# Moving the modulation products of a two-block, two-layer network between the feed-forward stages

## The chip, the cores and the metric

One core of a Trainium2 chip runs the whole program; TensorE (PE), VectorE (DVE), ScalarE (ACT), GpSimd (POOL) and SyncE (SP, which issues nearly all DMAs here) each work through a queue of their own. The metric is the device time of one execution in microseconds (us), smaller is better.

## The reference, cut to what matters

A first block of two layers (a state-space mixer with attention, memory attention, an FFN) works on 512 tokens of 1024 features; a second block of two layers works on its output `x` and on 256 context tokens. In the second block each layer's norms, gates and shifts are modulated by vectors that depend on the two conditioning vectors alone, and not on `x`:

```python
silu_c = jax.nn.silu(c)
silu_cc = jax.nn.silu(c_ctx)
for i in range(DEPTH):                      # DEPTH = 2
    mod = silu_c @ w_mod[i] + b_mod[i]      # w_mod[i]: 1024 x 6144
    mod_c = silu_cc @ w_mod[i] + b_mod[i]
    sh1, sc1, gt1, sh2, sc2, gt2 = jnp.split(mod[:, None, :], 6, axis=-1)
    ...
    h = modulate(rmsnorm_2(x, g_attn[i]), sh1, sc1)
    ...                                     # attention of this layer
    h = modulate(rmsnorm_2(x, g_ffn[i]), sh2, sc2)
    x = x + gt2 * conv_ffn(h, ...)
    if not last:
        ctx = ctx + gt2c * conv_ffn(hc, ...)   # the same weights, 256 columns
```

Both blocks' FFNs have 2816 hidden features: an up product to 5632, a three-tap convolution over positions, a gate, a down product. In the second block's first layer the FFN runs over `x` (512 columns) and the context (256 columns) with the same weights.

## The kernel before, in words

Everything is held feature-major: a tile is 128 features by 512 tokens. A float32 product is made of three passes: weights and activations are split into a high part and a low part, and `lin` (L304) runs high by high, high by low and low by high for each 128 rows. So 1024 input features by 512 columns are 24 matmuls, into one PSUM bank. `wload` loads a weight tile (`wr`, two buffers, issued by SP), ScalarE makes its high part (`wh`, three buffers, L314) and VectorE its low part (`wl`, three buffers, L331).

The modulation is not done on TensorE. `mod_steps(i, n0, n1)` is a generator: it loads the conditioning vectors (spread over all partitions) and takes their Silu, and then for each of 48 output tiles m and 2 halves e of the input loads 128 x 512 of `w_mod` and multiplies it with each of the two vectors. Of every eight products two are made on VectorE, which sums along the row in the same instruction (L1280); six are made on GpSimd (L1282), and ScalarE sums them later (L1260), `MLAG` products behind. Loads run `MPF` steps ahead. At the end of a layer's 96 steps the sums, the bias and the gains are put together in `mod[i]` and `G[i]`. In each layer i of the first block the generator of that layer is stepped by `step`: once for each output tile of the memory attention (`MSTEP[1]`), and after each up pair j of the FFN (`F1_MOD`: 2 in the first of the FFN's four parts, 5 in the others); what is left is run at the end of the FFN. So layer 0's modulation lies in the first block's first FFN and layer 1's in its second. These two stages are called the first FFNs here. `mod[0]` is first needed where the context is modulated at the end of layer 1's FFN.

The first FFNs (`ffn1`) work through 22 pairs j of up tiles (a value and a gate tile, 24 matmuls each), whose banks go around three tags L, S and PT of two banks each. The down products of a part are spread between the up products of the next one. For each up tile VectorE multiplies the bank with the norm, ScalarE does one tap, VectorE two more (L1181), then come Silu, the gate and the split.

The second block's FFN (`ffn2`) has three parts of 8, 7 and 7 pairs. In a part all up products come first: for each pair j, tile e and stream s (context, then `x`) a `lin` into a bank of tag L (two banks; four with S for the first two pairs), and `conv`: ScalarE copies the bank, VectorE does all three taps (L2021 and L2023). After the part's last gate the eight output tiles of the down product follow for both streams (L2080 adds them to `x` and the context). At the end of layer 0's, `mod[1]` and `G[1]` are needed for the norm of layer 1.

Activations, modulation weights and products all share one set of 59 buffers (tag A). The order of the instructions within an engine is set by a planner from the order in the program and the buffers and data that are free.

Of the kernel before, what the change touches and what calls it, by code (L numbers as in the profile page):

```python
# [14 lines left out]
AF = mybir.ActivationFunctionType  # L15
# [19 lines left out]
SA = 'g'  # L35
SQT = 'sq'
PSTEP = (5,3,1)
MSTEP = (0,1,4,1,2)
MDN = (0,0,2)
MH = 48  # L40
MLAG = 3
FX = 1
FD = 3
MK = 2
# [15 lines left out]
EV3 = 1  # L60
EV2 = 1
PIN = 1
MPF = 4
MODV = (0,4)
WP = 0
FA0 = 1
# [18 lines left out]
LAGS = (3,5)  # L85
FF_PARTS = ((0, 8), (8, 7), (15, 7))
F1_PARTS = ((0, 6), (6, 6), (12, 5), (17, 5))
F1_MOD = (2, 5, 5, 5)
F1_KEEP = 2
FTAGS = ("L", "S", "PT")  # L90

# [167 lines left out]
class Builder:  # L259
# [802 lines left out]
    def mem_attn(self, i, f, mh, K, fn):  # L1062
        nc, a = self.nc, self.a
        rm = []
        o = []
        qs, pts = {}, {}

        V = []

        def prep(h, ds=(0, 1)):  # L1070
            for d in ds:
                ps = self.p("L")
                self.lin(ps, self.wload(a[f"w_mq{i}"][2 * h + d]), f.rhs)
                if not rm:
                    rm.append(self.rstd_of(f.acc, D))
                t = self.t("A", [P, S])
                nc.vector.scalar_tensor_tensor(out=t, in0=ps, scalar=256.0 ** -0.5, in1=rm[0], op0=ALU.mult, op1=ALU.mult)
                qs[h, d] = self.split(t)

        self.steps = self.mod_steps(i, 0, 96)  # L1080
        mv = self.mem_v(i, mh, V)
        for h in range(2):
            for d in range(2):
                next(mv)
                next(mv)
                prep(h, (d,))
                self.step(2 * h + d, MSTEP[0])
        next(mv, None)

        def unit(h, qt):  # L1090
            u = Builder.Feed()
            s = slice(qt * P, qt * P + P)

            def s1():
                sp = self.p("S")
                for d in range(2):
                    kh, kl = K[2 * h + d]
                    qh, ql = qs[h, d]
                    self.mm(sp[:, :ML], qh[:, s], kh, d == 0, False)
                    self.mm(sp[:, :ML], qh[:, s], kl, False, False)  # L1100
                    self.mm(sp[:, :ML], ql[:, s], kh, False, d == 1)
                self.sm1(u, sp[:, :ML], ML)

            def s2():
                self.sm2(u, ML)
                if EV3:
                    turned()

            def turned():
                if qt % 2 == 0:  # L1110
                    pts[h, qt // 2] = self.t("A", [P, 2, 2, P], F32R), self.t("A", [P, 2, 2, P], F32R)
                ph, pl = (z[:, :, qt % 2] for z in pts[h, qt // 2])
                v = u.pt[:, :ML].rearrange("p (k q) -> p k q", k=2)
                self.hi(ph, v)
                self.lo(pl, v, ph)

            def s3():
                if not EV3:
                    turned()
                if qt < 3:  # L1120
                    return
                for d in range(2):
                    op = self.p("O")
                    c0 = (2 * h + d) * P
                    for hf in range(2):
                        oh = op[:, hf * ML:hf * ML + ML]
                        for kb in range(2):
                            vh, vl = V[c0 // 512][kb]
                            cs = slice(c0 % 512, c0 % 512 + P)
                            ph, pl = (z[:, kb].rearrange("p a q -> p (a q)") for z in pts[h, hf])  # L1130
                            self.mm(oh, vh[:, cs], ph, hf == 0 and kb == 0, False)
                            self.mm(oh, vh[:, cs], pl, False, False)
                            self.mm(oh, vl[:, cs], ph, False, hf == 1 and kb == 1)
                    o.append(self.split(op))

            return s1, s2, s3

        units = [unit(h, qt) for h in range(4) for qt in range(4)]
        self.pipe(units, {4 * h: (lambda h=h: prep(h)) for h in range(2, 4)}, 5, *XLAGS)
        for m in range(KD):  # L1140
            ps = self.p("L")
            self.lin(ps, self.wload(a[f"w_mo{i}"][m]), o)
            self.mark_d = nc.vector.tensor_add(out=self.x[:, m], in0=self.x[:, m], in1=ps)
            self.feed(fn, m)
            self.step(m, MSTEP[1])


    def step(self, n, r):
        for _ in range(int((n + 1) * r) - int(n * r)):
            with self.after(PIN):  # L1150
                next(self.steps, None)
# [3 lines left out]
    def ffn1(self, i, f, fn):  # L1155
# [2 lines left out]
        rf = []  # L1158
        self.wp = WP
        self.bank = 0  # L1160

        def bank():
            self.bank += 1
            return self.p(FTAGS[self.bank % len(FTAGS)])

        def up(j):
            ab = []
            for e in range(2):
# [72 lines left out]
        self.G = [[self.c([P, KD, 2], name=f"G{i}{j}") for j in range(2)] for i in range(DEPTH)]  # L1241


    def mod_steps(self, i, n0, n1):
        nc = self.nc
        cv = []
        for v in range(2):
            for e in range(2):
                c = self.t("A", [P, 512])
                nc.sync.dma_start(out=c, in_=self.a["cvec"][v, e])  # L1250
                nc.scalar.activation(c, c, AF.Silu)
                cv.append(c)
            yield
        part = self.mparts
        late = []

        def add(k):
            while len(late) > k:
                o, t = late.pop(0)
                nc.scalar.activation(t, t, AF.Copy, accum_out=o)  # L1260

        ws = {}

        def load(n):
            if n < n1:
                ws[n] = self.t("A", [P, 512])
                nc.sync.dma_start(out=ws[n], in_=self.a["w_mod"][i, n // 2, n % 2])

        for n in range(n0, n0 + MPF):
            load(n)  # L1270
        for n in range(n0, n1):
            load(n + MPF)
            m, e = divmod(n, 2)
            w = ws.pop(n)
            for v in range(2):
                t = self.t("A", [P, 512])
                self.modn += 1
                o = part[:, v, e, m:m + 1]
                if self.modn % 8 in MODV:
                    nc.vector.scalar_tensor_tensor(out=t, in0=w, scalar=1.0, in1=cv[2 * v + e], op0=ALU.mult, op1=ALU.mult, accum_out=o)  # L1280
                else:
                    nc.gpsimd.tensor_mul(out=t, in0=w, in1=cv[2 * v + e])  # L1282
                    late.append((o, t))
            add(MLAG)
            yield
        add(0)
        if n1 == 96:
            for v in range(2):
                mo = self.mod[i][:, :, v]
                nc.vector.tensor_add(out=mo, in0=part[:, v, 0], in1=part[:, v, 1])  # L1290
                nc.vector.tensor_add(out=mo, in0=mo, in1=self.v(f"b_mod{i}"))
            for j, gn in ((0, "g_attn"), (1, "g_ffn")):
                for s in range(2):
                    nc.vector.scalar_tensor_tensor(out=self.G[i][j][:, :, s], in0=self.mod[i][:, 24 * j + 8:24 * j + 16, s], scalar=1.0,
                                                   in1=self.v(f"{gn}{i}"), op0=ALU.add, op1=ALU.mult)
            yield
# [699 lines left out]
    def ffn2(self, i, rx, rc, acc, accc, steps=iter(()), late=None):  # L1996
# [3 lines left out]
        if rc is not None:  # L2000
            streams[1] = (rc, ML)
        w, ab = {}, {}

        def up(j, e, s, tag="L"):
            rhs, n = streams[s]
            if (j, e) not in w:
                w[j, e] = self.wload(a[f"w_up2{i}"][j, e])
            ps = self.p(tag)
            self.lin(ps[:, :n], w[j, e], rhs)
            conv(j, e, s, ps)  # L2010

# [17 lines left out]
            ve.tensor_mul(out=A, in0=A, in1=B)  # L2029
            return self.split(A)  # L2030

        for pi, (j0, nj) in enumerate(FF_PARTS):
            act = {s: [] for s in streams}
            last = pi == len(FF_PARTS) - 1
            first = 0
            if pi == 0 and rc is not None and FX:

                for j, e, s in ((0, 0, 1), (0, 1, 1), (1, 0, 1), (0, 0, 0), (0, 1, 0), (1, 1, 1), (1, 0, 0), (1, 1, 0)):
                    up(j, e, s, "S" if s else "L")
                    if e == 1:  # L2040
                        act[s].append(gate(j, s))
                first = 2
# [13 lines left out]
            for j in range(j0 + first, j0 + nj):  # L2056
                for e in range(2):
                    if (j, e, 0) in ab:
                        continue
                    for s in sorted(streams, reverse=True):  # L2060
                        up(j, e, s)
                for s in sorted(streams, reverse=True):
                    act[s].append(gate(j, s))

            def weights(m):
                if m not in w:
# [5 lines left out]
            def down(m, s):  # L2072
# [1 line left out]
                if (m, s) in pss:  # L2074
                    ps = pss[m, s]
                else:
                    ps = self.p("L")
                    self.lin(ps[:, :n], weights(m), act[s])
                dst = self.cx(m) if s else self.x[:, m]
                ve.scalar_tensor_tensor(out=dst, in0=ps[:, :n], scalar=self.msl(i, 5, m, s), in1=dst, op0=ALU.mult, op1=ALU.add)  # L2080
# [6 lines left out]
                order = [(m, s) for m in range(KD - FD) for s in (0, 1)] + [(m, s) for s in (0, 1) for m in range(KD - FD, KD)]  # L2087
            w.clear()
            for z, (m, s) in enumerate(order[:DW]):
                pss[m, s] = self.p(DT2[z % len(DT2)])  # L2090
            self.lins([(pss[m, s][:, :streams[s][1]], weights(m), act[s]) for m, s in order[:DW]])
            for n, (m, s) in enumerate(order):
                down(m, s)
# [126 lines left out]
```

## Time and profile before

| | |
|---|---|
| median of 3 runs | 3871.4 us (3862.74 to 3874.72) |
| the profiled execution | 3872.89 us, span 3871.1 us |
| mean granted TensorE clock | 0.985 |
| TensorE busy | 3736.8 us, 97% |
| VectorE busy | 2664.9 us, 69% |
| ScalarE busy | 1832.7 us, 47% |
| GpSimd busy | 1004.3 us, 26% |
| DMA | 354.39 MB, mean 92 GB/s |

A stage is read as a stretch of the span: each engine's busy time in it, and the granted clock of TensorE as a share of its full speed. "Idle before" an instruction names what the engine waited for. First FFN of layer 0: 678 to 1088 us from the span's start; of layer 1: 1735 to some 2140; the second block's first FFN: some 2620 to 3170; its second: some 3468 to the end.

### The profile page before, as it was taken

To read this page: it belongs to the slowest core of one execution; us is meant where nothing else is said; L and a number is where in the kernel's file an instruction comes from. 1 tells how busy PE (TensorE), PEld (TensorE's weight loads), DVE (VectorE), ACT (ScalarE), POOL (GpSimd) and SP (SyncE) were. 2 spreads that over 40 slices of the span, in tenths; PEclk is the share of its full clock that TensorE was granted. 3 is DMA by queue.
4 is the path that set the end of the run, shared out by engine and by line. 5 is a ranking of instruction groups with operands and counts; after the bars stand their busy time and mean duration, and the time that the engine had idled before them with its cause. 6 is when DMAs were issued, how large, how long until landed. Compare 5 with 4: busy or idle time off the path is not lost. (4 is left out here: it accounts for less than half of the span.)

```text
span 3871.1 us, 55512 instructions
## 1 busy us (share of the span) xinstructions
PE 3736.8 (97%) x21300; PEld 3078.2 (80%) x21300; DVE 2664.9 (69%) x4579; ACT 1832.7 (47%) x3512; POOL 1004.3 (26%) x692
## 2 busy tenths in 40 slices
PE   8999999999999999999999999999999999999999
PEld 6777788777778777887777899778888888878887
DVE  7767656799977676668988753667545547657555
ACT  5645634455555455344555554664222224544232
POOL 1223243466621121234765112321000012100000
PEclk9999999999999999999999999999999999999999
DMA  3222132344422211333544433312212212012332
GB/s 111 66 77 64 47 125 99 112 153 158 147 90 66 77 55 51 126 102 106 169 159 138 130 99 95 104 59 71 66 61 62 64 55 73 15 39 89 97 93 93
DMA packets 128714, 354.39 MB, mean 92 GB/s; under 512 B 14144, under 2 KB 26816, under 8 KB 128448
## 3 DMA queue, kind: packets, MB, share of 16 engines
q1 hardware_dynamic: 127440, 349.62, 28.3%
q8 instruction: 168, 2.75, 0.3%
q10 hardware_dynamic: 1008, 1.21, 0.1%
q14 instruction: 98, 0.80, 0.1%
HBM read 346.58 MB, written 4.19 MB: 91 GB/s over the span
## 5 line engine op out<-in xcount | busy, mean ns | idle before, releaser
L304 PE MATMUL L<-A,wh 128*128 128x512 f32 (+1 forms) x6408 | 1867.0, 375 | 19.6 <-ACT wh L314 6.3
L304 PEld LDWEIGHTS L<-A,wh 128*128 128x128 f32 x6408 | 1149.5, 189 | 247.2 <-issue 14.0
L304 PE MATMUL L<-A,wl 128*128 128x512 f32 (+1 forms) x3204 | 1196.4, 374 | 16.2 <-DVE wl L331 15.4
L314 ACT ACTIVATE wh<-wr 128x1024 fp32r<-128x1024 f32 (+4 forms) x562 | 562.1, 1001 | 806.5 <-PE L L304 439.0
L331 DVE TENSOR_TENSOR wl<-wr,wh 128x1024 fp32r<-128x1024 f32 (+4 forms) x503 | 658.8, 1311 | 327.4 <-ACT wh L314 319.5
L304 PEld LDWEIGHTS L<-A,wl 128*128 128x128 f32 x3204 | 605.7, 189 | 133.3 <-DVE wl L331 21.2
L1282 POOL TENSOR_TENSOR A<-A,A 128x512 f32<-128x512 f32 x288 | 483.3, 1710 | 278.3 <-DMA A<-in_w_mod 129.0
L304 PE MATMUL S<-A,wh 128*128 128x512 f32 (+1 forms) x944 | 304.0, 403 | 21.9 <-ACT wh L314 12.1
L331 POOL TENSOR_TENSOR wl<-wr,wh 128x1024 fp32r<-128x1024 f32 (+1 forms) x59 | 139.7, 2368 | 564.3 <-ACT wh L314 479.2
L304 PE MATMUL L<-wh,A 128*128 128x256 f32 x1440 | 274.3, 286 | 2.6 <-ACT A L1307 2.0
L304 PE MATMUL PT<-A,wh 128*128 128x512 f32 (+1 forms) x904 | 263.4, 377 | 0.0
L304 PE MATMUL O<-A,A 128*64 128x128 f32 (+3 forms) x2528 | 235.2, 290 | 3.8 <-DVE A L648 3.6
L304 PEld LDWEIGHTS S<-A,wh 128*128 128x128 f32 x944 | 182.4, 196 | 67.9 <-ACT wh L314 13.8
L1181 DVE SCALAR_TENSOR_TENSOR A<-A,vec,A 128x512 f32<-128x512 f32 x176 | 214.9, 1221 | 29.9 <-ACT A L1179 26.0
L304 PEld LDWEIGHTS L<-wh,A 128*128 128x128 f32 x1440 | 227.1, 190 | 9.6 <-issue 5.3
L433 POOL TENSOR_TENSOR acc<-acc,A 128x512 f32<-128x512 f32 (+1 forms) x44 | 53.5, 1216 | 679.1 <-ACT A L427 677.3
L304 PEld LDWEIGHTS O<-A,A 128*64 128x64 f32 (+1 forms) x2528 | 169.3, 144 | 55.3 <-issue 32.1
L304 PE MATMUL L<-wl,A 128*128 128x256 f32 x720 | 205.3, 285 | 6.5 <-DVE wl L331 6.4
L304 PE MATMUL S<-A,wl 128*128 128x512 f32 (+1 forms) x472 | 190.6, 404 | 16.9 <-DVE wl L331 16.6
L1260 ACT ACTIVATE A<-A 128x512 f32<-128x512 f32 x288 | 177.3, 618 | 37.6 <-POOL A L1282 37.6
L304 PEld LDWEIGHTS PT<-A,wh 128*128 128x128 f32 x904 | 167.5, 192 | 33.1
L314 ACT ACTIVATE A<-A 128x512 fp32r<-128x512 f32 (+2 forms) x202 | 115.2, 570 | 152.7 <-DVE A L1184 77.9
(323 smaller groups left out, 5281.3 us busy)
## 6 DMA issues: line engine op xcount, KB each, us to landing
wr<-in_w_up SPq DMA_DIRECT2D x176, 512.0 KB
A<-in_w_mod SPq DMA_DIRECT2D x192, 256.0 KB
wr<-in_w_qkv SPq DMA_DIRECT2D x62, 512.0 KB
wr<-in_w_in SPq DMA_DIRECT2D x60, 512.0 KB
wr<-in_w_down SPq DMA_DIRECT2D x32, 448.0 KB
wr<-in_w_down SPq DMA_DIRECT2D x32, 384.0 KB
wr<-in_w_down SPq DMA_DIRECT2D x32, 320.0 KB
wr<-in_w_os SPq DMA_DIRECT2D x16, 512.0 KB
```

The lines of the kernel that those rows point to most:

```text
L304: self.last_mm = self.nc.tensor.matmul(out, lhsT=l, rhs=r, start=start, stop=stop, skip_group_check=True)
L314: self.nc.scalar.activation(h, src, AF.Copy)
L331: eng.tensor_sub(out=l[:, :cols], in0=r[:, :cols], in1=h[:, :cols].bitcast(F32))
L433: self.mark_p = (add or nc.gpsimd).tensor_add(out=acc.t, in0=acc.t, in1=dst)
L1181: ve.scalar_tensor_tensor(out=ac, in0=u[:, tap:tap + S], scalar=cw(tap), in1=ac, op0=ALU.mult, op1=ALU.add)
L1260: nc.scalar.activation(t, t, AF.Copy, accum_out=o)
L1282: nc.gpsimd.tensor_mul(out=t, in0=w, in1=cv[2 * v + e])
```

## The change

The modulation of layer 0 is split: its first 24 output tiles are made in the memory attention and FFN of layer 0, the other 24 in those of layer 1, at half the rate. The modulation of layer 1 moves to the second block's first FFN: after each up product from the third pair j on, `step` is called at a rate of 1.2 (4.8 steps for each j), and what is left is run before the last part's down products. There loads run 2 steps ahead instead of 4. Within a call of `mod_steps` the loop over the two halves is now the outer one, so two vectors are held at a time instead of four; they are loaded by each of the three calls (12 loads instead of 8). The number of products and their shares of the engines stay.

The second block's first FFN (where the context is there, `both`) gets four parts of 6, 6, 5 and 5 pairs instead of three, and its banks go around the tags L, S and PT. The second block's last FFN keeps its parts and its tag L.

```diff
-MSTEP = (0,1,4,1,2)
+MSTEP = (0,0.5)
-MLAG = 3
+MLAG = (3, 3)
-MPF = 4
+MPF = (4, 2)
-F1_MOD = (2, 5, 5, 5)
+F1_MOD = (1, 2.5, 2.5, 2.5)
+F2_PARTS = ((0, 6), (6, 6), (12, 5), (17, 5))
+M2STEP = 1.2
...
-        self.steps = self.mod_steps(i, 0, 96)
+        self.steps = self.mod_steps(0, 24 * i, 24 * i + 24)
...
+    def next_bank(self):
+        self.bank += 1
+        return self.p(FTAGS[self.bank % len(FTAGS)])
...
-    def mod_steps(self, i, n0, n1):
+    def mod_steps(self, i, m0, m1):
...
+        for e in range(2):
+            cv = []
+            for v in range(2):
                 c = self.t("A", [P, 512])
                 nc.sync.dma_start(out=c, in_=self.a["cvec"][v, e])
                 nc.scalar.activation(c, c, AF.Silu)
                 cv.append(c)
...
+            for m in range(m0, m0 + MPF[i]):
+                load(m)
             yield
...
+            for m in range(m0, m1):
+                load(m + MPF[i])
+                w = ws.pop(m)
+                for v in range(2):
+                    t = self.t("A", [P, 512])
+                    self.modn += 1
+                    o = part[:, v, e, m:m + 1]
+                    if self.modn % 8 in MODV:
+                        nc.vector.scalar_tensor_tensor(out=t, in0=w, scalar=1.0, in1=cv[v], op0=ALU.mult, op1=ALU.mult, accum_out=o)
+                    else:
+                        nc.gpsimd.tensor_mul(out=t, in0=w, in1=cv[v])
+                        late.append((o, t))
+                add(MLAG[i])
+                yield
+            add(0)
+        if m1 == 48:
...
+        both = rc is not None
+        bank = self.next_bank if both else lambda: self.p("L")
+        fparts = F2_PARTS if both else FF_PARTS
+        if both:
+            self.bank = 0
+            self.steps = self.mod_steps(1, 0, 48)
...
-        for pi, (j0, nj) in enumerate(FF_PARTS):
+        for pi, (j0, nj) in enumerate(fparts):
...
                     for s in sorted(streams, reverse=True):
                         up(j, e, s)
+                        if both:
+                            self.step(4 * j + 2 * e + 1 - s, M2STEP)
...
+            if last and both:
+                self.step(0, 200)
```

## Rows read from the trace of the kernel before

**Rows 1.** The page's first part: busy time, share of the span, instructions.
```profile
PE 3736.8 (97%) x21300; PEld 3078.2 (80%) x21300; DVE 2664.9 (69%) x4579; ACT 1832.7 (47%) x3512; POOL 1004.3 (26%) x692
```
**Rows 2.** Stretches: length, busy us and count of each engine, clock, DMA share, GB/s.
```profile
2851.06:2934.97 83.91, 83.91 (x483) 73.39 (x482) 54.96 (x130) 28.70 (x51) 0.00 (x0) 1.00 0.20 63
2943.00:2990.00 47.00, 46.84 (x271) 40.80 (x271) 24.07 (x47) 11.63 (x19) 0.00 (x0) 1.00 0.21 60
782.00:1040.00 258.00, 244.97 (x1016) 194.83 (x1016) 236.80 (x280) 146.53 (x314) 177.92 (x105) 0.97 0.48 158
702.00:782.00 80.00, 77.54 (x324) 62.01 (x324) 66.81 (x90) 41.55 (x76) 30.10 (x18) 0.97 0.35 115
662.00:1078.00 416.00, 393.62 (x1628) 313.81 (x1627) 361.79 (x462) 221.84 (x458) 258.14 (x157) 0.96 0.43 141
...
2620.00:2810.00 190.00, 185.75 (x1046) 160.44 (x1045) 122.62 (x266) 66.05 (x108) 8.79 (x6) 0.99 0.22 67
2810.00:2990.00 180.00, 179.84 (x1029) 156.95 (x1028) 95.27 (x207) 48.05 (x78) 0.00 (x0) 1.00 0.20 62
```
**Rows 3.** Order of time on TensorE (start, length): first matmuls of products in the FFNs.
```profile
704.27 0.62 PE L304 MATMUL L<-A,wh 128*128 128x512 f32 x2
709.87 0.63 PE L304 MATMUL S<-A,wh 128*128 128x512 f32 x2
...
1088.42 0.62 PE L304 MATMUL L<-A,wh 128*128 128x512 f32 x2
...
1759.22 0.62 PE L304 MATMUL L<-A,wh 128*128 128x512 f32 x2
...
2153.19 0.28 PE L304 MATMUL L<-wh,A 128*128 128x256 f32 x1
```
**Rows 4.** TensorE's waits, 662 to 1078: us in total, times, longest.
```profile
PE S L304 <- DVE wl L331: 7.9, 3, 3.6
PE L L304 <- DVE wl L331: 4.7, 2, 3.0
```
**Rows 5.** TensorE's longest wait, 2620 to 3165.
```profile
PE L L304 <- DVE x L1941: 2.8, 1, 2.8
```
**Rows 6.** VectorE's groups, 782 to 1040: busy, mean ns, idle before.
```profile
L1181 DVE SCALAR_TENSOR_TENSOR A<-A,vec,A 128x512 f32<-128x512 f32 x57 | 72.9, 1278 | 11.0 <-ACT A L1179 10.1
L331 DVE TENSOR_TENSOR wl<-wr,wh 128x1024 fp32r<-128x1024 f32 x30 | 47.4, 1578 | 7.3 <-ACT wh L314 7.3
L1280 DVE SCALAR_TENSOR_TENSOR A<-A,A 128x512 f32<-128x512 f32 x35 | 46.8, 1365 | 0.0
```
**Rows 7.** VectorE's groups, 2620 to 3165.
```profile
L2023 DVE SCALAR_TENSOR_TENSOR A<-A,vec,A 128x512 f32<-128x512 f32 x88 | 65.9, 749 | 1.3
L331 DVE TENSOR_TENSOR wl<-wr,wh 128x1024 fp32r<-128x1024 f32 x52 | 63.7, 1226 | 71.4 <-ACT wh L314 70.4
```
**Rows 8.** Order of time on VectorE and GpSimd, 825 to 841.
```profile
825.29 0.68 DVE L1280 SCALAR_TENSOR_TENSOR A<-A,A 128x512 f32<-128x512 f32 x1
...
836.75 3.48 DVE L1181 SCALAR_TENSOR_TENSOR A<-A,vec,A 128x512 f32<-128x512 f32 x2
...
825.64 14.04 POOL L1282 TENSOR_TENSOR A<-A,A 128x512 f32<-128x512 f32 x8 [7.93 <-DMA A<-in_w_mod]
```
**Rows 9.** The same view in the attention of layer 1, 1383 to 1388.
```profile
1384.96 1.61 DVE L992 TENSOR_SCALAR A<-A,sm 128x512 f32<-128x512 f32 x1
...
1386.68 0.49 DVE L992 TENSOR_SCALAR A<-A,sm 128x512 f32<-128x512 f32 x1
...
1383.52 2.77 POOL L331 TENSOR_TENSOR wl<-wr,wh 128x1024 fp32r<-128x1024 f32 x1 [25.77 <-ACT wh L314]
```
**Rows 10.** Order of time in SP's queue.
```profile
1037.66 2.06 SPq L325 DMA_DIRECT2D wr<-in_w_down  x2
1039.81 1.81 SPq L1267 DMA_DIRECT2D A<-in_w_mod  x4
...
2810.26 109.52 SPq L325 DMA_DIRECT2D wr<-in_w_up  x14
```

More of the change, by code (lines that the diff above doesn't have):

```diff
@@ L1160, in ffn1 @@
         self.bank = 0
-        def bank():
-            self.bank += 1
-            return self.p(FTAGS[self.bank % len(FTAGS)])
+        bank = self.next_bank
         def up(j):
@@ L1241, in mod_prep @@
         self.G = [[self.c([P, KD, 2], name=f"G{i}{j}") for j in range(2)] for i in range(DEPTH)]
-    def mod_steps(self, i, n0, n1):
+    def mod_steps(self, i, m0, m1):
         nc = self.nc
[L1246 to L1253, printed above, removed]
         part = self.mparts
@@ L1260, in add, with load @@
                 nc.scalar.activation(t, t, AF.Copy, accum_out=o)
[L1262 to L1274, printed above, removed]
-            for v in range(2):
[L1276 to L1284, printed above, removed]
-            yield
-        add(0)
-        if n1 == 96:
+        for e in range(2):
+            cv = []
+            for v in range(2):
+                c = self.t("A", [P, 512])
+                nc.sync.dma_start(out=c, in_=self.a["cvec"][v, e])
+                nc.scalar.activation(c, c, AF.Silu)
+                cv.append(c)
+            ws = {}
+            def load(m):
+                if m < m1:
+                    ws[m] = self.t("A", [P, 512])
+                    nc.sync.dma_start(out=ws[m], in_=self.a["w_mod"][i, m, e])
+            for m in range(m0, m0 + MPF[i]):
+                load(m)
+            yield
+            for m in range(m0, m1):
[14 more added lines that the diff above has]
+        if m1 == 48:
             for v in range(2):
@@ L2002, in ffn2, with up @@
         w, ab = {}, {}
-        def up(j, e, s, tag="L"):
+        both = rc is not None
[4 more added lines that the diff above has]
+            self.steps = self.mod_steps(1, 0, 48)
+        def up(j, e, s):
             rhs, n = streams[s]
@@ L2007, in up @@
                 w[j, e] = self.wload(a[f"w_up2{i}"][j, e])
-            ps = self.p(tag)
+            ps = bank()
             self.lin(ps[:, :n], w[j, e], rhs)
@@ L2030, in gate @@
             return self.split(A)
-        for pi, (j0, nj) in enumerate(FF_PARTS):
+        for pi, (j0, nj) in enumerate(fparts):
             act = {s: [] for s in streams}
-            last = pi == len(FF_PARTS) - 1
+            last = pi == len(fparts) - 1
             first = 0
@@ L2038, in ffn2 @@
                 for j, e, s in ((0, 0, 1), (0, 1, 1), (1, 0, 1), (0, 0, 0), (0, 1, 0), (1, 1, 1), (1, 0, 0), (1, 1, 0)):
-                    up(j, e, s, "S" if s else "L")
+                    up(j, e, s)
                     if e == 1:
@@ L2076, in down @@
                 else:
-                    ps = self.p("L")
+                    ps = bank()
                     self.lin(ps[:, :n], weights(m), act[s])
@@ L2089, in ffn2 @@
             for z, (m, s) in enumerate(order[:DW]):
-                pss[m, s] = self.p(DT2[z % len(DT2)])
+                pss[m, s] = bank()
             self.lins([(pss[m, s][:, :streams[s][1]], weights(m), act[s]) for m, s in order[:DW]])
```

## The prediction

> **What bounds the kernel now.** I read the page's busy shares first, then the busy time by stage, then who waits on TensorE in the stages that change. TensorE is busy 97% of the span [rows 1], so time can only come from the few per cent in which it waits or runs at a lower clock, and it can only be lost by making it wait where it now doesn't.
>
> The stages differ [rows 2]. In the first FFN of layer 0 (662 to 1078; layer 1's is the same code) VectorE is busy 87%, GpSimd 62%, the granted clock averages 0.96, and TensorE is busy 394 of 416 us. In the second block's first FFN (2620 to 3170) GpSimd is nearly idle, VectorE busy 53 to 65%, and TensorE is busy to within a few us at clock 0.99 to 1.00. So the change moves load from two stages with losses to one without any.
>
> How much the first FFNs lose: a 24-matmul product of 512 columns takes 709.87 - 704.27 = 5.60 us at full pace [rows 3]. From 704.27 on, layer 0 has 64 such products left (66 in all: 44 up, and 8 x 22 x 3 down matmuls / 24 = 22; two are done), 358.4 us. The mixer's first product begins at 1088.42, so 384.2 us pass: 25.8 are lost. Layer 1: 1759.22 to 2153.19 is 394.0 us, 35.6 lost, but there the context's normalisation stands at the end; I count 26 as belonging to the FFN, as in layer 0. What is lost before 704.27, at the norm and the feeds of the start, I leave out here. TensorE's long waits in layer 0 are for the low half of a weight, made on VectorE [rows 4], 12.6 us; the rest of the 25.8 I put down to the lower clock (a mean of 0.97 from 702 to 1040 [rows 2]; of the two levels, 1.2 and 2.4 GHz, the lower one has its share here, in the second block's up phases none). In the second block's FFN the longest wait on TensorE is 2.8 us, once, at its start [rows 5].
>
> **The price of a product.** Each layer has 96 loads and 192 products: 144 on GpSimd (each then summed on ScalarE), 48 on VectorE. What a GpSimd product costs VectorE is read from two stages with the same instruction. Between 782 and 1040 VectorE's 512-element scalar_tensor_tensor takes 1278 ns and the 1024-element wl 1578 ns [rows 6]; with GpSimd idle they take 749 and 1226 [rows 7]. That is 57 x 0.529 + 30 x 0.352 + 35 x 0.616 (the products, against 749) = 62 us, on 105 GpSimd products [rows 2], 0.6 us each. But there part of GpSimd's work runs beside VectorE's PSUM reads and pauses. Where both queues are full (825.64 to 839.68) eight products take 14.04 us, 1.755 each, and VectorE's two operations at 836.75 take 3.48 us instead of 2 x 0.75: 1.0 us lost for each [rows 8]. They take turns. The tensor_scalar of the second block's convolution is no refuge: the same kind takes 0.49 us alone and 1.61 us when a GpSimd instruction runs, ending with it (1383.52 + 2.77) [rows 9].
>
> The Trainium skill (SBUF — State Buffer, section "SBUF: two separate sides") calls the pair of ports that VectorE and GpSimd share an exclusive lock, held for the whole instruction, with the loser blocked. This speaks against the change, and the trace agrees that they exclude each other; priced by GpSimd's recorded 1.755 us instead of the 1.0 us of the burst, the second block would lose some 109 us more (144 x 0.755). The recorded time holds GpSimd's own waiting, since VectorE's two operations end within it, so I stay with 1.0.
>
> **Part by part.** (1) First FFNs: steps and products per up product are halved (72 on GpSimd and 24 on VectorE in each stage). Between 782 and 1040 VectorE's 236.8 busy us [rows 2] fall by half of the 62 and half of 35 x 0.749 = 26, to 193, 75%. The stretch 702 to 782, with 2 steps instead of 5 per column pair, has 84% and TensorE busy 77.5 of 80 us; the second block's up phases at 65% lose nothing. So most of the 26 goes: I leave 3 in each stage and add 2 for the feeds at the start, where fewer products stand in GpSimd's queue before the sums of squares: 25 per stage, **50 us gained**. Its bounds: 36 (only the waits and half the clock go) to 60.
>
> (2) Second block's first FFN: 192 products come to 20 of the 22 column pairs j (4.8 steps each: 7.2 on GpSimd, 2.4 on VectorE), all in the up phases. Five j's run from 2851.06 to 2934.97: 16.78 us each, in which VectorE is busy 54.96 / 5 = 10.99 us [rows 2]; nearly all of it reads SBUF. With 2.4 x 0.68 us = 1.6 of products (0.68 is one between two neighbours without contention [rows 8]) and 7.2 x 1.0 for GpSimd's turns the sum is 19.8 us, 3.0 over TensorE's 16.78: 20 x 3.0 = 61 us. The chain behind it: wl, and the convolution and gate of the last j, are late; the down products at the end of a part need the gate of the last j, so the backlog of a part (4 to 6 j's, 12 to 18 us) becomes a wait of TensorE there. Six banks instead of two don't help: the wait is for weights and gated columns, not for a free bank. For the low clock after four such waits I add 2 us each: **69 us lost**. Bounds: 0, if the products run beside the down phases (VectorE busy 24 of 47 us there [rows 2]; over the whole 550 us VectorE's 123 + 95 + some 95, the products' 33 and the turns' 144 would fit), and 110, if pauses are not filled (4.4 over per j, and 5 us of clock for each of four waits).
>
> Do the products drift into the down phases? The weights do run ahead: the load of the second part's first up weight is issued at 2810.26 [rows 10], when the second part's own up products are still some 30 us off (weights are consumed 8.4 us apart, half of 16.78, and two raw and three split ones are held). But the modulation loads of layer 0 stand later: the last ones are issued at 1039.81, behind two down weights that the program names after them [rows 10]. That is not before their step's up product ends: back from 1088.42 lie eleven down products of 3.5 us, two up products of 5.6 and one more down, to 1035. So I take products at the pace of TensorE, not ahead.
>
> (3) Small parts: four parts instead of three mean 16 more down evacuations, 8 of 0.75 us [rows 7] and 8 of half the columns, some 10 us of VectorE in down phases that are half idle: nothing. Four more loads and Silu of the vectors: in cover, as ScalarE is at 27 to 35% there; in the first FFNs it sums the same 144 products and stays at 53%. SP's queue: 96 loads go past 88 weight loads, and a load waits for one of 59 buffers with the weight behind it; ends 0 and 20 us, I take 0, as with 28 long-lived tiles (24 of inputs, 4 of the context), 18 gated ones and about 10 of the steps some are left. The modulation of layer 0 now ends just before the context is modulated, ten down products ahead of TensorE's need: nothing. That of layer 1 is flushed before the last down phase: a few small VectorE operations beside 40 us of down products.
>
> **Sum.** 69 - 50 = +19. The profiled execution took 3872.9 us (span 3871.1), 1.5 above the median 3871.4; from the median the forecast is **3890**.
>
> **Rivals.** (a) The products fit into the down phases and VectorE's pauses: a third of the 61 remains and the wait at part ends is 1 us each: 24 lost, 50 gained, 3845. For it: 40% of VectorE's time is free there and weights run 30 us ahead; against it: the order of the loads at 1039.81, and that the products are tied to up steps. It decides if GpSimd is busy in the down phases. (b) Halfway, 69 becomes 45 to 55: about 3871, no change to be told. (c) The slower side beyond the forecast: a loaded buffer is late, SP's queue holds weights back (20), the turns leave pauses unfilled (110 instead of 69) and the first FFNs give 40: with 95 lost that is 3926. It decides when TensorE waits for weights whose DMA is late. (d) The change doesn't do what it says, that is the first FFNs keep their losses because they come from another source than the products (the norm, part ends): 15 gained, 3925. Against it: the waits are for VectorE, which is the busy engine there.
>
> **Chances.** Forecast 0.42, (c) and (d) 0.08 together, (b) 0.20, (a) 0.30. The bound for what a measurement of this kernel can tell is 0.3%, 11.6 us. The likeliest case's own range is 3876 to 3915; to hold eight in ten it must reach into (a) and (c): 3838 to 3928. Faster 0.30, same 0.20, slower 0.50.
>
> **What would show it.** In the changed kernel's first FFNs: clock 0.98 or more, VectorE near 75%, waits for wl under 5 us in each. In the second block's FFN: scalar_tensor_tensor of 512 at 1.2 us or more instead of 0.749, its span 600 us or more from the first to the last up and down weight instead of some 550, TensorE waiting for wl and for the gate at four places. The prediction is wrong if that stage keeps within 30 us of its old length, if GpSimd's products lie in the down phases, or if the first FFNs stay above 400 us.

## The result, and the profile after

The changed kernel takes 3902.8 us (median of 4 runs, 3894.24 to 3905.39) where the kernel before takes 3869.74 in the same comparison: ratio 1.0076, interval 1.006 to 1.0091, slower by 0.6 to 0.9%. The profiled execution's span is 3900.8 us, 29.7 more than before's 3871.1.

The page's first part of the changed kernel, to hold against [rows 1]:

```profile
PE 3724.6 (95%) x21300; PEld 3076.9 (79%) x21300; DVE 2681.3 (69%) x4603; ACT 1836.0 (47%) x3524; POOL 957.6 (25%) x692
```

The totals hardly move; the stages do. SP's queue (start, length) shows where they begin: the first weight of layer 1's mixer and the first up weight of the second block. First the changed kernel:

```profile
1048.06 0.33 SPq L327 DMA_DIRECT2D wr<-in_w_in  x1
...
2557.11 0.33 SPq L327 DMA_DIRECT2D wr<-in_w_up  x1
```

and the same two in the kernel before:

```profile
1077.73 0.33 SPq L325 DMA_DIRECT2D wr<-in_w_in  x1
...
2621.10 0.33 SPq L325 DMA_DIRECT2D wr<-in_w_up  x1
```

The first layer's end comes 29.7 us earlier, the second block's first FFN starts 64.0 us earlier, so layer 1 gave 34.3. How long that FFN takes is counted on TensorE, between the same two matmuls of both kernels: the sum for a norm in front of the FFN and the second such sum behind it (3312 matmuls; columns as in [rows 2]). First the kernel before, then the changed one:

```profile
2635.28:3213.77 578.49, 574.67 (x3313) 502.69 (x3314) 325.64 (x699) 172.29 (x280) 19.24 (x16) 1.00 0.21 63
...
2571.27:3243.55 672.28, 597.84 (x3313) 518.75 (x3314) 489.39 (x827) 260.65 (x580) 234.47 (x156) 0.93 0.29 93
```

It takes 93.8 us more, and from there to the end both kernels need the same time, 657.3 us. Together -64.0 + 93.8 = +29.8, the 29.7 of the span.

Stretches of the changed kernel (length, then busy us and count of TensorE, its weight loads, VectorE, ScalarE, GpSimd; then clock, DMA share, GB/s; columns as in [rows 2]):

```profile
702.00:1048.00 346.00, 346.00 (x1493) 280.04 (x1492) 260.09 (x366) 168.83 (x298) 102.08 (x67) 1.00 0.40 124
1740.00:2060.00 320.00, 320.00 (x1383) 259.47 (x1382) 245.02 (x350) 158.71 (x288) 92.99 (x60) 1.00 0.41 130
2557.11:3204.16 647.05, 572.95 (x3120) 493.87 (x3119) 477.61 (x804) 253.52 (x571) 234.30 (x155) 0.93 0.29 95
2680.00:2720.00 40.00, 23.90 (x119) 20.19 (x118) 26.91 (x47) 12.54 (x27) 10.95 (x8) 0.79 0.21 62
2800.00:2840.00 40.00, 39.80 (x231) 34.72 (x230) 36.72 (x59) 17.50 (x45) 20.06 (x14) 1.00 0.30 103
2840.00:2880.00 40.00, 21.96 (x99) 18.12 (x97) 35.06 (x62) 19.56 (x49) 17.71 (x12) 0.77 0.26 79
2880.00:2920.00 40.00, 39.96 (x213) 35.00 (x214) 13.71 (x21) 5.30 (x6) 0.00 (x0) 0.93 0.24 70
```

In the first FFNs TensorE no longer stops once they are under way: 346.00 of 346.00 us and 320.00 of 320.00 at clock 1.00, with VectorE at 75 and 77%. (Ahead of these two stretches it still waits once each for a norm, 7.9 and 6.9 us.) The third stretch runs from that FFN's first up weight to the first load behind it. In the second block's first FFN TensorE keeps its pace through the up products (2800 to 2840), while VectorE fills to 92%; then at the part's end (2840 to 2880) TensorE is busy 22 of 40 us at clock 0.77, and in the down phase GpSimd has nothing at all.

TensorE's waits in that FFN, 2557 to 3205 (us in total, times, longest), where [rows 5] had one of 2.8 us as the longest:

```profile
PE PT L306 <- ACT A L316: 29.4, 5, 10.9
PE S L306 <- DVE wl L333: 10.0, 3, 6.8
PE S L306 <- ACT A L316: 9.9, 1, 9.9
PE L L306 <- DVE wl L333: 9.1, 3, 5.3
PE PT L306 <- DVE A L319: 4.9, 2, 2.7
PE S L306 <- DVE A L319: 4.3, 2, 2.8
```

The gated column's high part (L316 on ScalarE, behind VectorE's gate) and low part (L319), and the weight's low half (L333). The longest of each part's end, in order of time:

```profile
2696.82 0.58 PE L306 MATMUL S<-A,wh 128*128 128x256 f32 x1 [9.85 <-ACT A L316]
...
2874.59 0.58 PE L306 MATMUL PT<-A,wh 128*128 128x256 f32 x1 [9.01 <-ACT A L316]
...
3030.86 0.58 PE L306 MATMUL PT<-A,wh 128*128 128x256 f32 x1 [10.88 <-ACT A L316]
...
3176.98 0.80 PE L306 MATMUL S<-A,wl 128*128 128x512 f32 x1 [6.76 <-DVE wl L333]
```

VectorE's groups there, to hold against [rows 7], and GpSimd's products:

```profile
L2033 DVE SCALAR_TENSOR_TENSOR A<-A,vec,A 128x512 f32<-128x512 f32 x88 | 90.0, 1023 | 1.2
L333 DVE TENSOR_TENSOR wl<-wr,wh 128x1024 fp32r<-128x1024 f32 x44 | 62.1, 1411 | 23.6 <-ACT wh L316 22.3
L1283 DVE SCALAR_TENSOR_TENSOR A<-A,A 128x512 f32<-128x512 f32 x48 | 48.6, 1013 | 2.8 <-ACT wh L316 2.8
...
L1285 POOL TENSOR_TENSOR A<-A,A 128x512 f32<-128x512 f32 x144 | 219.5, 1549 | 391.2 <-DMA A<-in_w_mod 241.7 <-ACT A L1263 62.8 <-DVE A L1283 23.8
```

The 512-element operation has gone from 749 to 1023 ns. GpSimd itself had time to spare: it sat idle 391 us before these products.

The 93.8 us can be divided by TensorE's busy time between the two matmuls. Before, it was busy 574.67 of 578.49 us, 3.8 idle; now it is 597.84 of 672.28, 74.4 idle (from 2557.11 to 3204.16, the stretch used below, it is 74.1). So 70.6 us are waits and 23.2 us longer matmuls. How much of the latter is the four parts and how much the clock, the first experiment tells.

### The profile page after: what moved, and what is told of

It is laid out like the page before. It is cut to its first block, busy times and chain, and to the rows that moved or that the text cites. A ratio compares the mean times of both kernels' runs of the same rounds, so it can differ in the third digit from the quotient of the medians.

```text
span 3900.8 us, 55505 instructions
## 1 busy us (share of the span) xinstructions
PE 3724.6 (95%) x21300; PEld 3076.9 (79%) x21300; DVE 2681.3 (69%) x4603; ACT 1836.0 (47%) x3524; POOL 957.6 (25%) x692
## 4 chain that ended last, share of the span: by engine, by line
PE 77%; DVE 14%; ACT 3%; issue 3%; DMA 1%; POOL 1%; SPq 0%; ACTq 0%; DVEq 0%; POOLq 0%
PE L L306 41%; PE S L306 16%; PE PT L306 9%; PE O L306 6%; DVE A L2033 2%; DVE wl L333 2%; DVE A L2031 2%; DVE A L319 1%; PE s L306 1%; ACT wh L316 1%; PE PT L997 1%; PE PT L1899 1%; DVE A L1283 1%; PE PT L1700 1%; DVE A L440 1%
## 5 line engine op out<-in xcount | busy, mean ns | idle before, releaser
L306 PE MATMUL L<-A,wh 128*128 128x512 f32 (+1 forms) x5060 | 1529.3, 384 | 17.5 <-DVE A L822 4.9
L306 PEld LDWEIGHTS L<-A,wh 128*128 128x128 f32 x5060 | 919.6, 190 | 209.8 <-issue 13.7
L306 PE MATMUL L<-A,wl 128*128 128x512 f32 (+1 forms) x2530 | 964.8, 382 | 13.8 <-DVE wl L333 13.2
L316 ACT ACTIVATE wh<-wr 128x1024 fp32r<-128x1024 f32 (+4 forms) x570 | 564.9, 992 | 877.4 <-PE L L306 353.0
L333 DVE TENSOR_TENSOR wl<-wr,wh 128x1024 fp32r<-128x1024 f32 (+4 forms) x511 | 637.1, 1248 | 251.3 <-ACT wh L316 240.3
L306 PEld LDWEIGHTS L<-A,wl 128*128 128x128 f32 x2530 | 480.1, 190 | 111.7 <-DVE wl L333 16.0
L306 PE MATMUL S<-A,wh 128*128 128x512 f32 (+1 forms) x1592 | 468.9, 378 | 25.7 <-ACT A L316 9.9
L306 PE MATMUL PT<-A,wh 128*128 128x512 f32 (+1 forms) x1604 | 438.0, 360 | 34.3 <-ACT A L316 29.4
L306 PEld LDWEIGHTS PT<-A,wh 128*128 128x128 f32 x1604 | 285.9, 190 | 85.4 <-ACT A L316 31.7
L306 PE MATMUL PT<-A,wl 128*128 128x512 f32 (+1 forms) x802 | 287.5, 358 | 1.9 <-DVE wl L333 1.9
L333 POOL TENSOR_TENSOR wl<-wr,wh 128x1024 fp32r<-128x1024 f32 (+1 forms) x59 | 139.1, 2357 | 569.2 <-ACT wh L316 494.3
L2033 DVE SCALAR_TENSOR_TENSOR A<-A,vec,A 128x512 f32<-128x512 f32 (+1 forms) x264 | 222.7, 845 | 5.2
L319 DVE TENSOR_TENSOR A<-A,A 128x512 fp32r<-128x512 f32 (+2 forms) x202 | 156.2, 774 | 43.7 <-ACT A L316 42.2
```

The source lines that it names most:

```text
L306: self.last_mm = self.nc.tensor.matmul(out, lhsT=l, rhs=r, start=start, stop=stop, skip_group_check=True)
L316: self.nc.scalar.activation(h, src, AF.Copy)
L319: self.nc.vector.tensor_sub(out=l, in0=src, in1=h.bitcast(F32))
L333: eng.tensor_sub(out=l[:, :cols], in0=r[:, :cols], in1=h[:, :cols].bitcast(F32))
L2033: ve.scalar_tensor_tensor(out=ac, in0=u[:, tap:tap + n], scalar=cw(tap), in1=ac, op0=ALU.mult, op1=ALU.add)
```

## The experiments

The theory after the result: VectorE takes turns with GpSimd, falls behind TensorE in the up phases, and the backlog comes due at the part ends. The rivals: the four parts and the banks, the loads and ScalarE's sums that moved along, and simply the amount of work.

**Parts and banks alone.** The kernel before, with the four parts and the rotating banks; no products moved.

```
-        for pi, (j0, nj) in enumerate(FF_PARTS):
+        for pi, (j0, nj) in enumerate(fparts):       # 6, 6, 5, 5
...
-            ps = self.p(tag)
+            ps = bank()                              # L, S, PT in turn
```

> The kernel before, with the second block's first FFN in four parts of 6, 6, 5 and 5 pairs and its banks in turn over three tags; all modulation products stay where they were before. Theory of turns (GpSimd's products and VectorE's convolution exclude each other in the up phases): no change, 3862 to 3882 us, TensorE's waits in that stage under 8 us. Rival of the parts (the 100 us that the stage got longer come from shorter parts, whose gates are less hidden, and from the bank order): 3900 to 3970 us.

Measured: 3878.16 us, ratio 1.0009 (0.9999 to 1.0019). The stage from its first up weight to the first load behind it, in the kernel before and here, and then between the same two matmuls as above:

```profile
2621.10:3168.49 547.39, 542.27 (x3073) 471.17 (x3072) 313.17 (x676) 165.21 (x271) 14.90 (x11) 1.00 0.21 64
...
2622.42:3175.85 553.43, 549.67 (x3120) 478.46 (x3119) 323.56 (x700) 167.18 (x279) 14.61 (x11) 1.00 0.21 63
...
2636.62:3215.75 579.13, 575.06 (x3313) 504.03 (x3314) 335.35 (x723) 174.26 (x288) 15.35 (x13) 0.99 0.21 63
```

Between the loads the stage looks 6 us longer, but with the new parts the load behind it is issued later in TensorE's work: 3120 matmuls lie in this stretch instead of 3073. Between the same two matmuls it takes 579.13 us against 578.49 before, 575.06 of them busy against 574.67. So parts and banks alone cost nothing that can be told, and the 23.2 us of longer matmuls are left for the low clock.

**GpSimd's products cut short.** In the changed kernel the second layer's GpSimd products cover 32 of 512 columns, while ScalarE still sums 512 columns (of the weights), so most of what GpSimd computes there is left out. Loads, instructions and sums stay.

```
...
-                        nc.gpsimd.tensor_mul(out=t, in0=w, in1=cv[v])
-                        late.append((o, t))
+                        k = 32 if i else 512
+                        nc.gpsimd.tensor_mul(out=t[:, :k], in0=w[:, :k], in1=cv[v][:, :k])
+                        late.append((o, t, w if i else t))
```

> The changed kernel, but layer 1's 144 GpSimd products are made on 32 of 512 columns (the rest is left out; ScalarE sums the loaded weights instead, behind the short product, so loads, buffers, sums and waits stay). Theory of turns: GpSimd holds VectorE up for a tenth of the time, the stage falls from 647 us to some 555 to 570, the kernel to 3810 to 3830 us. Rival of the plumbing (loads in SP's queue, the 59 buffers or ScalarE's sums make weights and gates late): no change, 3890 to 3910 us.

Measured: 3807.04 us, ratio 0.9823 (0.9809 to 0.9838), 3 us below the range that was expected. The stage, and VectorE's first group in it:

```profile
2555.93:3109.79 553.86, 550.31 (x3120) 478.69 (x3119) 353.96 (x804) 256.68 (x571) 69.79 (x155) 1.00 0.35 111
...
L2034 DVE SCALAR_TENSOR_TENSOR A<-A,vec,A 128x512 f32<-128x512 f32 x88 | 66.0, 752 | 1.3
```

The stage is as long as with no products at all (553.43, over the same 3120 matmuls), ScalarE as busy as in the changed kernel (256.68 and 253.52 us), and VectorE's operation is back at 752 ns. Loads, SP's queue, buffers and ScalarE's sums cost nothing; the columns that GpSimd works through cost all of it.

**The second layer's products on VectorE.** All 192 stay where the change put them, none on GpSimd.

```
-                    if self.modn % 8 in MODV:
+                    if i or self.modn % 8 in MODV:
```

> The changed kernel, but all 192 products of layer 1 are made and summed on VectorE, none on GpSimd. Theory of turns: VectorE needs 10.99 + 9.6 x 0.72 = 17.9 us for each pair against TensorE's 16.78, 1.1 too much instead of some 4: 20 to 25 us of waits and 10 to 20 of low clock, 3830 to 3850 us. Rival (VectorE is simply overloaded by the products it has itself, GpSimd's are free): 144 more products of 0.72 us on the engine that is late, 3980 to 4010 us. Rival of the plumbing: loads as before, the sums on ScalarE gone: 3800 to 3900 us without a change in the waits for wl.

Measured: 3807.43 us, ratio 0.9825 (0.981 to 0.9839): below the range that was expected. Three stretches, and VectorE's five largest groups in the last of them:

```profile
2551.33:3106.84 555.51, 550.92 (x3120) 478.38 (x3119) 428.96 (x1092) 168.60 (x283) 14.56 (x11) 1.00 0.34 110
2734.00:2800.00 66.00, 66.00 (x380) 57.73 (x379) 60.95 (x170) 22.96 (x40) 0.00 (x0) 1.00 0.39 127
2740.00:2800.00 60.00, 60.00 (x343) 52.36 (x342) 56.31 (x156) 20.69 (x36) 0.00 (x0) 1.00 0.40 131
...
L1283 DVE SCALAR_TENSOR_TENSOR A<-A,A 128x512 f32<-128x512 f32 x34 | 23.1, 685 | 0.0
L2033 DVE SCALAR_TENSOR_TENSOR A<-A,vec,A 128x512 f32<-128x512 f32 (+1 forms) x27 | 16.7, 620 | 0.0
L333 DVE TENSOR_TENSOR wl<-wr,wh 128x1024 fp32r<-128x1024 f32 x7 | 8.6, 1221 | 0.2 <-ACT wh L316 0.2
L2031 DVE TENSOR_SCALAR A<-A,vec 128x512 f32<-128x512 f32 (+1 forms) x14 | 6.7, 478 | 0.6
L319 DVE TENSOR_TENSOR A<-A,A 128x256 fp32r<-128x256 f32 (+1 forms) x8 | 4.5, 557 | 2.1 <-ACT A L316 2.1
```

VectorE does four times as many products here, TensorE doesn't wait, and the products cost the stage 2 us over no products at all. Two things follow. The five groups add up to 59.6 us in a stretch in which VectorE was busy 56.31: recorded lengths overlap, so an instruction's mean length is more than its price. And the price can be read from the busy time: 60.95 of 66 us is 15.5 us for a column pair of 16.78, against 54.96 / 5 = 11.0 without products [rows 2], so 4.5 us for 9.6 products, **about 0.5 us each** where the record says 0.685. The Trainium skill (Perfetto Trace Analysis, section "Optimizing Scalar/DVE Operations") says that part of a VectorE instruction's profiled latency overlaps with the next instruction; the sum of these rows agrees.

**The same products, spread.** Six of eight on GpSimd as in the change, but stepped through the down phases too.

```
-M2STEP = 1.2
+M2STEP = 0.65
+M2DOWN = 0.75
...
                 down(m, s)
+                if both and (n < 9 or not last):
+                    self.step(n, M2DOWN)
...
```

> The changed kernel with the same products, but 0.65 steps after each up product and 0.75 after each down product instead of 1.2 and none; the rest is run after the tenth of the last part's sixteen down products. Theory of turns: 2.6 steps for each pair are 10.99 + 2.6 x 1.86 = 15.8 us of VectorE and turns against 16.78, so the waits at the part ends mostly go: 3810 to 3835 us. Rival of the parts, and rival of the plumbing (same loads, sums and buffers): no change, 3890 to 3910 us.

Measured: 3835.74 us, ratio 0.9898 (0.9884 to 0.9913), just over the upper edge.

```profile
2551.97:3131.03 579.06, 562.30 (x3146) 488.01 (x3145) 435.21 (x793) 252.55 (x559) 225.52 (x149) 0.98 0.33 105
...
L2034 DVE SCALAR_TENSOR_TENSOR A<-A,vec,A 128x512 f32<-128x512 f32 x88 | 73.4, 835 | 1.3
```

TensorE's idle time in this stretch falls from 74.1 to 16.8 us with not one product taken away (behind the stretch it waits once more, 5.4 us, for a sum that GpSimd makes). So the changed kernel's loss hung on the crowding into the up phases; yet spread out, GpSimd's products still cost 28 us more than VectorE's own.

**Half and half.** That gives a second theory, of prices: making a product costs VectorE 0.5 us, letting GpSimd make it about twice that. The test is a dose between 0 and 144: every second product of the second layer on GpSimd, 96.

```
-                    if self.modn % 8 in MODV:
+                    if self.modn % 8 in ((0, 2, 4, 6) if i else MODV):
```

> The changed kernel with half of the second layer's products on VectorE (96) and half on GpSimd (96), instead of 48 and 144. Price theory (0.5 us for VectorE's own product, 1.0 to 1.1 for GpSimd's turn): a column pair needs 11.0 + 4.8 x 0.5 + 4.8 x 1.05 = 18.4 us of VectorE for TensorE's 16.8, 1.6 over, half of what the changed kernel lacks (11.0 + 2.4 x 0.5 + 7.2 x 1.05 = 19.8, 3.0 over): some 33 us of waits at the part ends and 13 of low clock, 3840 to 3865 us, between the 3807 with none on GpSimd and the 3903 with 144. Rival (what the products cost VectorE is the same on either engine, and only the recorded lengths count): 3885 to 3905. Rival (a part's VectorE products can be put off and GpSimd's cannot, so that anything under the full load fits): 3805 to 3825.

Measured: 3863.07 us, ratio 0.9974 (0.9964 to 0.9984), inside the theory's range, near its upper end, and outside both rivals'.

```profile
2558.00:3170.00 612.00, 566.90 (x3119) 491.03 (x3118) 456.10 (x900) 224.76 (x475) 157.67 (x107) 0.95 0.31 100
```

The price worked back from the idle time, over the 4.6 us (555.51 - 550.92) that are there without GpSimd: 45.1 - 4.6 = 40.5 us over 20 column pairs, 2.0 each, so 16.78 + 2.0 = 11.0 + 4.8 x 0.5 + 4.8 x g, and g = 1.12 us. For the changed kernel: (74.1 - 4.6) / 20 = 3.5, 16.78 + 3.5 = 11.0 + 2.4 x 0.5 + 7.2 x g, g = 1.12. Two doses, one price, somewhat less than GpSimd's recorded 1549 ns and over twice VectorE's own. That the loss follows this sum at 0, 96 and 144 products is measured; that the price is the wait for a port is inferred from the stretched lengths, no run shows the port.

Two limits of the sum. For the spread version's up phases it gives 11.0 + 1.3 x 0.5 + 3.9 x 1.12 = 16.0 us, under the 16.78, and yet TensorE stood idle in that stage, 16.8 us against 4.6. And the two prices aren't read alike: 0.5 is VectorE's busy time, while 1.12 counts all the time that passes, and VectorE isn't busy all of it. The changed kernel's second part, from its first up product's taps to its last one's:

```profile
2754.10:2877.90 123.80, 106.79 (x582) 92.08 (x581) 108.09 (x180) 57.12 (x145) 63.33 (x42) 0.93 0.32 108
```

That is 108.09 / 6 = 18.0 us of VectorE's busy time for a column pair, so (18.0 - 11.0 - 1.2) / 7.2 = 0.8 us for a GpSimd product by the measure that gives 0.5 for VectorE's own; the rest of the 1.12 is time in which VectorE is idle.

**The kernel before, all on VectorE.** Nothing moved: the products stay in the first FFNs.

```
-                if self.modn % 8 in MODV:
+                if True:
```

> The kernel before, with nothing moved, but all 192 products of each layer on VectorE and none on GpSimd. Price theory: what GpSimd's product costs VectorE by its turns (about 1.0 us) is twice what the product costs VectorE when it makes it itself. That own price is read from the earlier run with all second-layer products on VectorE: between 2734 and 2800 it is busy 60.95 of 66 us, 15.5 for each column pair against 11.0 without products, for 9.6 products, so about 0.5 us each. In the first FFNs 782 to 1040 VectorE's 236.8 us lose 105 turns at some 0.65 (that stage's price, from its fall to 260 of 346 us when half the products left) and gain 105 x 0.5: some 221 of 258, 86%, and at 93% TensorE did not wait in that run. So the first FFNs lose their waits and their low clock with nothing moved: 50 to 64 us gained, 3805 to 3825 us. Rival (the place is what counts, the products have to leave the first FFNs): by the recorded length of 0.69 + 0.08 us VectorE has 256 of 258 us to do, weights stay late, and the time is 3860 to 3900.

Measured: 3797.35 us, ratio 0.9804 (0.9786 to 0.9822), better than expected. The stretch of [rows 2], and its products:

```profile
782.00:1040.00 258.00, 256.55 (x1105) 207.00 (x1104) 240.00 (x527) 90.64 (x116) 8.29 (x6) 1.00 0.50 162
...
L1280 DVE SCALAR_TENSOR_TENSOR A<-A,A 128x512 f32<-128x512 f32 x146 | 90.8, 688 | 0.0
```

VectorE is busier than before (240.0 of 258 us against 236.8; 221 were expected, but the stretch now holds 1105 matmuls instead of 1016), and TensorE, which had lost 13 us in this stretch, loses 1.5 at clock 1.00 instead of 0.97. A VectorE at 92% was not full of work: by the prediction's sum 62 us of it were waiting for GpSimd's turns. The products did not have to leave the first FFNs.

**All on VectorE, placed as in the change.**

```
-                    if self.modn % 8 in MODV:
+                    if True:
```

> The changed kernel with all products of both layers on VectorE, none on GpSimd. Price theory: the first FFNs already show no waits and a clock of 1.00 with half the products on GpSimd, so there is nothing left to gain there; VectorE goes there from 75% to about 78%; 3800 to 3812 us, the same as with only the second layer's products on VectorE (3807.4). Rival (VectorE becomes the engine that holds the first FFNs): waits for wl come back, 3820 to 3850.

Measured: 3791.22 us, ratio 0.9786 (0.9771 to 0.98), below the theory's range: 16 us less than with only the second layer's products on VectorE, where the theory saw nothing left to gain. What had been left is at the first FFNs' beginnings. With only the second layer's products on VectorE, as in the changed kernel, TensorE waits there once for the norm's reciprocal root, in layer 0 and in layer 1 (around 690 and 1720):

```profile
PE O L306 <- DVE rt L381: 7.9, 1, 7.9
...
PE O L306 <- DVE rt L381: 6.9, 1, 6.9
```

and here, in layer 0:

```profile
PE O L306 <- DVE rt L381: 0.2, 1, 0.2
```

In layer 1 no such wait is left.

By the medians this is the fastest kernel of the study, though its interval overlaps that of the kernel before with all products on VectorE.

**Products moved, parts and banks as before.**

```
-        bank = self.next_bank if both else lambda: self.p("L")
-        fparts = F2_PARTS if both else FF_PARTS
+        bank = lambda: self.p("L")
+        fparts = FF_PARTS
...
```

> The changed kernel with the second block's first FFN in its old three parts of 8, 7 and 7 column pairs and on banks of tag L, the products placed as in the change. Price theory: the backlog of 20 column pairs is the same, some 65 us, and comes due at three part ends instead of four, with a low clock after three: 3885 to 3905 us, within 0.5% of the changed kernel (3902.8), and TensorE's long waits at three places. Rival (the four parts and the three tags help, by spreading the backlog or by banks that let TensorE run on): 3915 or more.

Measured: 3887.63 us, ratio 1.0032 (1.0019 to 1.0045): in the range, but not in the way expected. The stage, an up phase, and TensorE's main wait:

```profile
2555.00:3184.00 629.00, 567.04 (x3073) 483.70 (x3073) 455.58 (x780) 253.74 (x563) 233.49 (x156) 0.97 0.31 98
...
2880.00:2920.00 40.00, 35.72 (x194) 30.84 (x193) 35.76 (x66) 20.47 (x48) 18.02 (x11) 0.96 0.40 134
...
PE L L306 <- ACT A L2028: 52.9, 30, 3.6
```

With two banks TensorE cannot run ahead of the conversion chain: it stops thirty times for a bank, at most 3.6 us, instead of at four part ends for some 17 us each (70.6 / 4). The idle time is 62.0 us instead of 74.1. Parts and tags didn't make the loss; they moved it to the part ends, and it grew a little there.

**All on VectorE, parts and banks as before**, meant as the fastest version: the two edits above together.

> The changed kernel with all products of both layers on VectorE (3791.2 us), and the second block's first FFN back in its three parts of 8, 7 and 7 column pairs on banks of tag L. Price theory: VectorE needs some 15.6 of the 16.8 us of a column pair, so TensorE has nothing to wait for on two banks either, and the fourth part's 6 us (553.4 against 547.4 us of that stage, with no products in it) are saved: 3782 to 3790 us, VectorE at 90 to 95% in the up phases. Rival (two banks don't cover VectorE at such a load: short waits of TensorE for the bank, as the 30 that summed to 52.9 us with the products on GpSimd): 3800 to 3830 us.

Measured: 3800.11 us, ratio 0.9815 (0.9798 to 0.9831): 10 us above the theory's range, at the lower edge of the rival's. The stage between the same two matmuls, with all products on VectorE in the change's parts and here, and two of the waits here:

```profile
2550.21:3131.57 581.36, 576.23 (x3312) 504.25 (x3313) 440.72 (x1114) 175.96 (x292) 14.70 (x12) 0.99 0.33 108
...
2547.11:3140.49 593.38, 580.37 (x3312) 504.29 (x3313) 432.13 (x1091) 173.54 (x284) 19.22 (x16) 0.99 0.33 106
...
PE L L306 <- ACT A L2028: 4.3, 4, 1.5
PE L L306 <- DVE x L2095: 2.8, 1, 2.8
```

TensorE is idle 13.0 us instead of the 5.1 of four parts and three tags, and the stage is 12 us longer. The 6 us that three parts were to save are not there: they came from stretches with different numbers of matmuls, 3073 and 3120. With all products on VectorE the change's parts and banks together are worth some 9 us by the medians; but the two versions were timed in different comparisons, and their intervals just touch (0.9771 to 0.98, 0.9798 to 0.9831).

## Why the prediction was right, and where its steps were off

The forecast was 3890, the measured time 3902.8, and the side (slower) is right by the mechanism named: less load in two stages that stumbled, and in a third a backlog of VectorE that becomes TensorE's wait at four part ends. Both large terms came out too small, by 14 and by 25 us, and their errors partly cancel: that the total is off by only 13 us is in part luck.

**First FFNs: 50 gained by the forecast, 64.0 measured**, beyond its bound of 60. Layer 0 gave 29.7 instead of 25, since all of its loss went and some of what the start had lost. Layer 1 gave 34.3. The step that failed is the count of 26 for layer 1 out of 35.6, which left out 10 us at its end as belonging to the context's normalisation. Between the two matmuls of that count (1759.22 and 2153.19 before, 1727.03 and 2087.21 now) 33.8 us came back. The first sum for the norm, before and now, stands at

```profile
2125.47 0.58 PE L304 MATMUL O<-ones,acc 128*128 128x1 f32 x4 [2.20 <-DVE acc L433]
...
2060.66 0.58 PE L306 MATMUL O<-ones,acc 128*128 128x1 f32 x4
```

so 32.6 of the 33.8 lay ahead of it: the 10 us were lost in the FFN itself and not at the norm.

What was to show there came: clock 1.00, VectorE at 75%, no wait for wl in 662 to 1048, where [rows 4] had 12.6 us. The rival that the losses have another source falls with it.

**Second block's first FFN: 69 lost by the forecast, 93.8 measured**, inside its bounds. The backlog's 61 stands against 70.6 us of waits, at the four places named: its sum of 19.8 us for a column pair was made of two errors of opposite sign, VectorE's own product at 0.68 us (0.5 measured) and GpSimd's turn at 1.0 (1.12), and by the measured ones is 20.3 (the 1.12 is worked back from these waits; what confirms it is the half dose). The low clock's 8 us, 2 for each wait with no row behind them, are the term that was mis-sized most: it took 23.2, more than even the 5 us a wait of the bound, with 0.77 to 0.79 granted in the 40 us around a part end. The four parts, put at nothing because VectorE has room in the down phases, did cost nothing (579.13 us against 578.49).

One sign that was to come didn't: the 512-element operation went to 1.02 us, not to 1.2 or more. Its lengthening, (1.023 - 0.749) x 88, is 24 us; that of all of VectorE's groups in the stage is some 122 us, 0.85 for each of GpSimd's 144 products. That agrees with the 0.8 by VectorE's busy time.

**Small parts.** SP's queue, the longer row of loads, the buffers and ScalarE's sums were put at nothing with an end of 20 us (the loads pass 76 weight loads there, not 88); the run with short products shows nothing for all of them together. The rival that slower loads add to the loss falls with it.

**Drift into the down phases** (the rival of 3845): GpSimd's 0.00 us from 2880 to 2920 says that the products keep to TensorE's pace, as the order of the loads had said [rows 10]. How large that gain would have been, the spread version shows: 3835.74.

**What the prediction didn't ask** is whether GpSimd helps at all. It took GpSimd's turn (1.0) and VectorE's own product (0.68) into one sum and had the larger number stand for the helper: 144 x 1.0 us of turns to save VectorE 144 x 0.68 us of work. The rows for that were at hand [rows 8]. The Trainium skill (Perfetto Trace Analysis, section "Optimizing Scalar/DVE Operations") warns that moving work between GpSimd and VectorE might not help, since they share a read port; here it did worse than that, 3791 to 3797 us without the helper, and 3870 and 3903 with it.

## What to carry to other kernels

Before work is moved to a helper engine, compare what the helper's instruction costs the busy engine with what the work costs there: here 0.8 us of its busy time, 1.12 with the idle time that came with it, against 0.5 for the same product, so that taking GpSimd's help away gained 2 to 3%, wherever the products lay. A busy share of 92% may be in good part blocked time; whether the engine is full shows only when the blocker is gone. And when load is moved out of one stage into another with room on average, look at the phase it lands in: crowded into the up phases it cost 94 us, spread over up and down phases some 30. And a stage's cost is compared between the same two matmuls: between two loads, 6 us of it were only a load issued later.

## What the runs showed that was not expected

- VectorE's recorded lengths overlap: five groups sum to 59.6 us within 56.31 busy us, and a product of 685 ns adds only about 0.5 us of busy time.
- VectorE at 92% of a stretch (60.95 of 66 us) holds nothing up so long as GpSimd is still, while in the changed kernel 36.72 of 40 us already meant a backlog.
- The same products cost less as many short waits for a bank (30, 3.6 us at most, clock 0.96 in that phase) than as a few long ones at part ends (clock 0.77 to 0.79 around them): 62.0 against 74.1 us idle. TensorE's busy time grew by about as much in both, 25 us (567.04 - 542.27, 3073 matmuls each) and 23, so the clock doesn't explain the difference.
